# VectorE in the order of the source over a whole two-layer encoder

## The chip, the cores and the metric

One core of one Trainium2 chip runs one program that holds the whole two-layer encoder. The time is that of the device in microseconds (us), from launch to end. Weights are read from HBM as float32 and each is used as the sum of two rounded parts, so the matrix work is three (sometimes two wider) passes for every product.

## What is computed

A residual stream of 16 learned tokens and 256 tokens (T = 272 columns) of width 2048 goes through two layers:

```
h = RMSNorm(x);  [q|k|v|f|ga|gf] = h @ W_in
a = attention(q, k, v) @ W_attn_br          # 8 heads, 2 key/value heads
s = Re(DFT2(f)) @ W_four                    # fourier branch
x = x + (sigmoid(ga)*a + sigmoid(gf)*s) @ W_out
x = x + W_down( silu(dwconv3(RMSNorm(x) @ W_up_gate)) * (RMSNorm(x) @ W_up_val) )
```

The 16 tokens are dropped at the end. The feed-forward width is 5632.

## The kernel before, in words

All weights pass through one stream of **chunks** of 128x1024 float32 (512 KB each), numbered 0 to 947 in the order of use. For a chunk, SyncE issues the load into a tile `raw` (seven buffers, L264); ScalarE writes the rounded high part `wh` (L300); VectorE writes the rest `wl` = `raw` - `wh` (L303); TensorE reads both. `wh` and `wl` have three buffers each, so at most two chunks lie ready ahead of the one in use, and the two parts of chunk n+3 can be written only when TensorE has read chunk n. The `raw` buffer of chunk n is free when its `wl` is done, and then chunk n+7 can be loaded.

The chunks of one matrix group (`group`, L346) follow each other. Names of groups: `ga`, `gf` (gates, 4 chunks), `s` (fourier branch, 2 chunks), `a` (attention branch, 2), `o` (output projection, 2), `ug` and `uv` (the two halves of the feed-forward's first matrix, 4 each), `d` (its second, 5 or 6). In a normal chunk TensorE does 24 matmuls: for each of 8 weight blocks two that read `wh` and then one that reads `wl` (L372, L373, L374). In layer 1 the feed-forward also has chunks of **products** (`ps_p`, L1415): six matmuls of 512 columns, four that read `wh` and then two that read `wl`. They stand singly, in pairs or in threes between the chunks of `ug` and `uv`.

In layer 0, each of the two chunks of an `s` group is first **folded** on VectorE: half of it is added to and subtracted from the other half (`fold_w`, L291, two instructions, into the single buffer `wpm`), and `wh` and `wl` are made from `wpm`. There are eight such groups.

Behind each `ug` group stands the **conv chain** (`conv_gate`, L1246), for each of the group's two halves m: `u` (VectorE, L1255, frees the accumulator), `cv` (ScalarE, L1257), two steps of the convolution (VectorE, L1259 and L1260), silu (ScalarE, L1261), and in layer 0 a product with the norm (VectorE, L1263):

```
nc.vector.tensor_tensor(hv(u[:, lo:T]), de(ps[m][:, :W]), ...)                     # L1255
nc.scalar.activation(cv[:, lo2:T], u[:, lo2:T], AF.Identity, bias=bc, scale=wc(1)) # L1257
nc.vector.scalar_tensor_tensor(cv[:, a:T], u[:, a - 1:T - 1], wc(0), ...)          # L1259
nc.vector.scalar_tensor_tensor(cv[:, lo2:T - 1], u[:, lo2 + 1:T], wc(2), ...)      # L1260
nc.scalar.activation(cv[:, lo2:T], cv[:, lo2:T], AF.Silu)                          # L1261
nc.vector.tensor_tensor(cv, cv, rstdB, op=ALU.mult)                                # L1263
```

After an `o` group of the second half and after the last `d` groups stands a **norm step** for each of two tiles: the sum into the residual stream (VectorE, L1236 or L1286), the scaled copy and the square (ScalarE, L517 and L523), the low part and the running sum of squares (VectorE, L518 and L527).

The source writes the splits of chunk n+2 between the matmuls of chunk n (`pump`, `advance`), and attention, fourier transforms and norms run as generators that are stepped between the matmuls (`step`). A scheduler then sets the order of the instructions of each engine from the dependencies and its own estimates; the source's order is only its priority. Two stretches (the group `f` 2 of layer 0, and the group `q` 1 with the folded fourier projection of layer 1) are already kept in the order of the source on VectorE. Every engine takes its instructions strictly in the order that it has been given, and waits on semaphores where an operand is not ready.

## Time and profile before

| | before |
|---|---|
| median of three runs | 2420.45 us (2418.58 to 2429.65) |
| the profiled execution's own time | 2423.76 us |
| its span, first to last instruction | 2421.7 us |
| TensorE busy | 2375.5 us, 18992 matmuls |
| VectorE busy | 1818.4 us, 2889 instructions |
| ScalarE busy | 1308.3 us, 1893 instructions |
| mean granted clock of TensorE | 0.994 |

The profile tells each instruction's line, engine and tiles (out<-in, with buffer numbers left out), how long an engine sat idle before it and which engine's instruction ended that wait. A window is a stretch of the span in us from its start. In the windows' table "PE busy" is TensorE and PEclk the share of full speed that its clock was granted.

### The profile page before, as it was taken

What the parts mean: (1) busy time and instruction counts of PE and PEld (TensorE: products, weight loads), DVE (VectorE), ACT (ScalarE), POOL (GpSimd) and SP (SyncE); (2) the same over time, 40 slices, a digit from 0 to 9 for tenths busy, and PEclk for the clock granted to TensorE, in tenths of its full rate; (3) what the DMA queues carried; (4) which work ended last, traced back from release to release, by engine and by line L of the source; (5) the groups of instructions that cost most, each with busy time, mean ns of one, the idle gap of its engine ahead of it and who ended that gap; (6) DMA issues with size and microseconds to landing.
All of it is one profiled execution on the core that took longest, in us unless ns stands there. A gap on an engine that the chain in (4) does not pass through costs nothing.

```text
span 2421.7 us, 47634 instructions
## 1 busy us (share of the span) xinstructions
PE 2375.5 (98%) x18992; PEld 2315.1 (96%) x18992; DVE 1818.4 (75%) x2889; ACT 1308.3 (54%) x1893; POOL 134.0 (6%) x265
## 2 busy tenths in 40 slices
PE   9999899999999999999999999999999999999999
PEld 9999899999999999999998999999989999999988
DVE  7788666687776656677668877766878888878798
ACT  6455444464444434444445655545677566666565
POOL 0000010100000000000000000000000000000000
PEclk9999899999999999999999999999999999999999
DMA  7547898899999999999885646888889989988787
GB/s 276 175 155 237 244 288 264 269 298 309 311 315 335 313 306 333 300 343 319 271 261 166 204 156 196 269 265 271 286 290 312 317 281 318 298 299 277 260 279 251
DMA packets 171215, 660.69 MB, mean 273 GB/s; under 512 B 19424, under 2 KB 24672, under 8 KB 170096
## 3 DMA queue, kind: packets, MB, share of 16 engines
q1 hardware_dynamic: 152528, 538.07, 63.9%
q0 software_dynamic: 17024, 117.45, 19.3%
q8 instruction: 149, 2.44, 0.4%
q10 hardware_dynamic: 1440, 2.13, 0.2%
q14 instruction: 74, 0.61, 0.1%
HBM read 635.91 MB, written 136.31 MB: 319 GB/s over the span
## 4 chain that ended last, share of the span: by engine, by line
PE 88%; DVE 6%; DMA 3%; ACT 2%; issue 1%; POOL 0%; SPq 0%; DVEq 0%; ACTq 0%; POOLq 0%
PE ps_p L1415 9%; PE ps_ug L374 7%; PE ps_ug L373 6%; PE ps_ug L372 6%; PE ps_uv L368 4%; PE ps_d L373 3%; PE ps_uv L374 3%; PE ps_d L372 3%; PE ps_uv L372 3%; PE ps_uv L373 3%; PE ps_d L374 3%; DVE wl L303 3%; PE ps_o L372 2%; PE ps_o L373 2%; PE ps_o L374 2%; PE ps_gf L372 2%
## 5 line engine op out<-in xcount | busy, mean ns | idle before, releaser
L303 DVE TENSOR_TENSOR wl<-raw,wh 128x1024 fp32r<-128x1024 f32 (+1 forms) x937 | 1127.0, 1217 | 460.0 <-ACT wh L300 452.1
L300 ACT CAST wh<-raw 128x1024 fp32r<-128x1024 f32 (+1 forms) x937 | 965.7, 1042 | 762.5 <-PE ps_ug L373 197.9
L374 PE MATMUL ps_ug<-xHL,wl 128*128 128x272 f32 (+1 forms) x1408 | 390.8, 278 | 2.2 <-DVE wl L303 2.1
L372 PE MATMUL ps_ug<-xHL,wh 128*128 128x272 f32 (+1 forms) x1408 | 390.8, 278 | 0.2 <-ACT wh L300 0.2
L373 PE MATMUL ps_ug<-xHL,wh 128*128 128x272 f32 (+1 forms) x1408 | 390.0, 277 | 0.0
L374 PEld LDWEIGHTS ps_ug<-xHL,wl 128*128 128x128 f32 x1408 | 267.5, 190 | 3.3 <-DVE wl L303 3.1
L372 PEld LDWEIGHTS ps_ug<-xHL,wh 128*128 128x128 f32 x1408 | 267.3, 190 | 2.7 <-ACT wh L300 0.6
L373 PEld LDWEIGHTS ps_ug<-xHL,wh 128*128 128x128 f32 x1408 | 267.4, 190 | 2.1
L372 PE MATMUL ps_uv<-xHL,wh 128*128 128x272 f32 x704 | 196.4, 279 | 0.0
L373 PE MATMUL ps_uv<-xHL,wh 128*128 128x272 f32 x704 | 196.4, 279 | 0.0
L374 PE MATMUL ps_uv<-xHL,wl 128*128 128x272 f32 x704 | 196.4, 279 | 0.0
L372 PE MATMUL ps_d<-gHL,wh 128*128 128x272 f32 x704 | 196.4, 279 | 0.0
L373 PE MATMUL ps_d<-gHL,wh 128*128 128x272 f32 x704 | 196.4, 279 | 0.0
L374 PE MATMUL ps_d<-gHL,wl 128*128 128x272 f32 x704 | 196.4, 279 | 0.0
L1415 PE MATMUL ps_p<-wh,opnd 128*128 128x512 f32 x688 | 177.5, 380 | 0.3 <-ACT wh L300 0.3
L374 PE MATMUL ps_ga<-xHL,wl 128*128 128x272 f32 (+1 forms) x512 | 144.9, 283 | 10.9 <-DVE wl L303 10.9
L372 PE MATMUL ps_ga<-xHL,wh 128*128 128x272 f32 (+1 forms) x512 | 146.6, 286 | 4.5 <-DVE se L1207 4.5
L368 PE MATMUL ps_uv<-xHL,wh 128*128 128x512 f32 x448 | 150.8, 383 | 0.1
L372 PE MATMUL ps_gf<-xHL,wh 128*128 128x272 f32 (+1 forms) x512 | 144.9, 283 | 5.1 <-DVE se L1207 4.9
L373 PE MATMUL ps_ga<-xHL,wh 128*128 128x272 f32 (+1 forms) x512 | 144.4, 282 | 0.0
L373 PE MATMUL ps_gf<-xHL,wh 128*128 128x272 f32 (+1 forms) x512 | 143.1, 280 | 0.0
L374 PE MATMUL ps_gf<-xHL,wl 128*128 128x272 f32 (+1 forms) x512 | 143.1, 279 | 0.0
(372 smaller groups left out, 5857.2 us busy)
## 6 DMA issues: line engine op xcount, KB each, us to landing
raw<-in_w_up SPq DMA_DIRECT2D x320, 512.0 KB, 5.6
raw<-in_w_in SPq DMA_DIRECT2D x191, 512.0 KB, 4.5
raw<-in_w_down SPq DMA_DIRECT2D x88, 512.0 KB, 7.0
raw<-ft SPq DMA_DIRECT2D x80, 512.0 KB, 4.8
raw<-in_w_out SPq DMA_DIRECT2D x64, 512.0 KB, 5.7
ft<-in_w_dn POOLq DMA_DIRECT2D x30, 1024.0 KB, 12.3
raw<-in_w_dn SPq DMA_DIRECT2D x60, 512.0 KB, 5.0
raw<-in_w_abr SPq DMA_DIRECT2D x32, 512.0 KB, 4.7
```

Source lines behind the costliest of these rows:

```text
L300: nc.scalar.copy(h[:, a:b], r[:, a:b])
L303: nc.vector.tensor_tensor(lo[:, a:b], r[:, a:b], h[:, a:b].bitcast(F32), op=ALU.subtract)
L368: nc.tensor.matmul(o2, h[:, c, sl], ab, start=kt == 0, stop=False)
L372: nc.tensor.matmul(o, h[:, c, sl], a, start=kt == 0, stop=False)
L373: nc.tensor.matmul(o, h[:, c, sl], b, start=False, stop=False)
L374: nc.tensor.matmul(o, lo[:, c, sl], a, start=False, stop=kt == nk - 1)
L1415: nc.tensor.matmul(st2(ps[h]), x, al(w[:, 512 * h:512 * h + 512]), start=fresh and (s_, q) in BEGIN and first, stop=(s_, q) in END and end ...
```

## The change

One line is put around the call that writes the whole program: VectorE (DVE) takes its instructions in the order in which the source writes them. The orders of TensorE, ScalarE, GpSimd and SyncE are still found by the scheduler, which now sees the fixed order on VectorE.

```
     with tile.TileContext(nc) as tc:
-        encoder_kernel(tc, *args)
+        with tc.manual_schedule(engines={mybir.EngineType.DVE}):
+            encoder_kernel(tc, *args)
```

No instruction is added or taken away; 2493 of VectorE's 2891 instructions stand at another place than before, most of them by fewer than ten places. Three places follow; the numbers behind `wl`, `wh`, `raw` and `wpm` are the chunk's, those behind an underscore the buffer's name.

First, VectorE in layer 0 around the second fourier group `s` 1 (chunks 72 and 73); chunk 80 is the first of the next `s` group, seven chunks later. Before:

```order
L303 TENSOR_TENSOR wl73_3395<-wpm73_3385,wh73_3394 128x1024
L1227 TENSOR_TENSOR th_2123<-th_2123,th_2948 128x272
L1226 SCALAR_TENSOR_TENSOR th_2123<-th_2123,ps_0_a_0_1_3340 128x272
L291 TENSOR_TENSOR wpm80_3633<-raw80_3374 128x512
L1229 TENSOR_TENSOR mL_3338<-th_2123,mH_3337 128x272
L1227 TENSOR_TENSOR th_2123<-th_2123,th_2948 128x272
L303 TENSOR_TENSOR wl74_3427<-raw74_3177,wh74_3426 128x1024
```

and with the change, the same stretch:

```order
L303 TENSOR_TENSOR wl73_3397<-wpm73_3387,wh73_3396 128x1024
L1226 SCALAR_TENSOR_TENSOR th_2125<-th_2125,ps_0_a_0_0_3341 128x272
L1227 TENSOR_TENSOR th_2125<-th_2125,th_2950 128x272
L1229 TENSOR_TENSOR mL_3340<-th_2125,mH_3339 128x272
L1226 SCALAR_TENSOR_TENSOR th_2125<-th_2125,ps_0_a_0_1_3342 128x272
L1227 TENSOR_TENSOR th_2125<-th_2125,th_2950 128x272
L1229 TENSOR_TENSOR mL_3340<-th_2125,mH_3339 128x272
L303 TENSOR_TENSOR wl74_3429<-raw74_3179,wh74_3428 128x1024
```

and, further on, the place to which the fold of chunk 80 went:

```order
L303 TENSOR_TENSOR wl79_3599<-raw79_3343,wh79_3598 128x1024
L1184 TENSOR_TENSOR th_3620<-ps_0_gf_3_0_3495,rstdB_82 128x272
L1184 TENSOR_TENSOR th_3620<-ps_0_gf_3_1_3496,rstdB_82 128x272
L291 TENSOR_TENSOR wpm80_3635<-raw80_3376 128x512 x2
L303 TENSOR_TENSOR wl80_3645<-wpm80_3635,wh80_3644 128x1024
L291 TENSOR_TENSOR wpm81_3671<-raw81_3420 128x512 x2
```

The fold of chunk 80 stood ahead of the low part of chunk 74; now it stands behind that of chunk 79, next to the split of chunk 80 itself.

Second, VectorE in the feed-forward of layer 0, behind `ug` group 5 (its last chunk is 211; 212 and 213 are the two that lie ready, 214 is the next). Before:

```order
L303 TENSOR_TENSOR wl213_8310<-raw213_8071,wh213_8309 128x1024
L1255 TENSOR_TENSOR u_8331<-ps_0_ug_5_0_8201,rstdB_80 128x272
L1255 TENSOR_TENSOR u_8339<-ps_0_ug_5_1_8202,rstdB_80 128x272
L1259 SCALAR_TENSOR_TENSOR cv_8333<-u_8331,prm_71,cv_8333 128x271
L1260 SCALAR_TENSOR_TENSOR cv_8333<-u_8331,prm_71,cv_8333 128x271
L303 TENSOR_TENSOR wl214_8361<-raw214_8102,wh214_8360 128x1024
L1263 TENSOR_TENSOR cv_8333<-cv_8333,rstdB_80 128x272
```

and with the change:

```order
L303 TENSOR_TENSOR wl213_8312<-raw213_8073,wh213_8311 128x1024
L1255 TENSOR_TENSOR u_8333<-ps_0_ug_5_0_8203,rstdB_82 128x272
L1259 SCALAR_TENSOR_TENSOR cv_8335<-u_8333,prm_73,cv_8335 128x271
L1260 SCALAR_TENSOR_TENSOR cv_8335<-u_8333,prm_73,cv_8335 128x271
L1263 TENSOR_TENSOR cv_8335<-cv_8335,rstdB_82 128x272
L1255 TENSOR_TENSOR u_8341<-ps_0_ug_5_1_8204,rstdB_82 128x272
L1259 SCALAR_TENSOR_TENSOR cv_8343<-u_8341,prm_73,cv_8343 128x271
L1260 SCALAR_TENSOR_TENSOR cv_8343<-u_8341,prm_73,cv_8343 128x271
L1263 TENSOR_TENSOR cv_8343<-cv_8343,rstdB_82 128x272
L303 TENSOR_TENSOR wl214_8363<-raw214_8104,wh214_8362 128x1024
```

The low part of chunk 214 stood in the middle of the chain of the first half; now the whole chain of both halves stands ahead of it.

Third, ScalarE in the feed-forward of layer 1, behind `ug` group 2 (its last chunk is 636, the next are 637 and 638, both products, and 639, of `uv`). Its order is the scheduler's in both. Before:

```order
L300 CAST wh638_23208<-raw638_23024 128x1024
L1257 ACTIVATE cv_23232<-u_23230,prm_71 128x256
L300 CAST wh639_23252<-raw639_23043 128x1024
L1257 ACTIVATE cv_23239<-u_23237,prm_71 128x256
L1261 ACTIVATE cv_23232<-cv_23232 128x256
L300 CAST wh640_23264<-raw640_23073 128x1024
```

and with the change:

```order
L300 CAST wh638_23210<-raw638_23026 128x1024
L1257 ACTIVATE cv_23234<-u_23232,prm_73 128x256
L300 CAST wh639_23254<-raw639_23045 128x1024
L300 CAST wh640_23266<-raw640_23075 128x1024
L1261 ACTIVATE cv_23234<-cv_23234 128x256
L1257 ACTIVATE cv_23241<-u_23239,prm_73 128x256
```

The cast of chunk 640 moved ahead of the second half's `cv`, for which VectorE's chain waits; on VectorE the low part of chunk 639, which stood behind the first half's L1260, now stands behind the second half's.

## The prediction

> **What bounds the kernel now.** The page first.

> ```profile
> span 2421.7 us, 47634 instructions
> ...
> PE 2375.5 (98%) x18992; PEld 2315.1 (96%) x18992; DVE 1818.4 (75%) x2889; ACT 1308.3 (54%) x1893; POOL 134.0 (6%) x265
> ```

> TensorE (PE) is busy for all but 46 us, so it is the bound, and a change on VectorE (DVE) can only take away TensorE's waits or add to them. Where they lie is shown by the windows by stage (three of the fourier groups in layer 0, then the feed-forward of layer 0 and of layer 1; columns as named in the first row):

> ```profile
> core 0: us, PE busy (x) PEld busy (x) DVE busy (x) ACT busy (x) POOL busy (x), PEclk, DMA share, GB/s
> 242.00:302.50 60.50, 51.09 (x402) 50.77 (x401) 40.63 (x70) 25.13 (x40) 4.91 (x10) 0.89 0.84 245
> 363.00:423.50 60.50, 55.25 (x450) 54.84 (x448) 37.21 (x64) 26.89 (x39) 4.22 (x10) 0.94 0.84 264
> 423.50:484.00 60.50, 54.84 (x457) 54.64 (x458) 41.71 (x64) 27.01 (x41) 8.10 (x12) 0.97 0.88 267
> 541.00:1155.00 614.00, 614.00 (x5302) 613.96 (x5302) 417.83 (x625) 284.59 (x353) 41.00 (x88) 1.00 0.96 318
> 1755.00:2421.70 666.70, 658.90 (x4261) 606.84 (x4259) 553.76 (x707) 429.39 (x556) 17.76 (x26) 1.00 0.86 289
> ```

> Of the 46 us, 20.3 (9.4 + 5.25 + 5.65) lie in the three fourier windows, where the clock was also granted below 1. The feed-forward of layer 0 loses nothing, that of layer 1 7.8 us in 667. The waits say who is late:

> ```profile
> PE ps_ga L374 <- DVE wl L303: 10.9, 3, 4.9
> PE ps_gf L372 <- DVE se L1207: 4.9, 1, 4.9
> ```

> ```profile
> DVE wpm L291 <- DMA raw<-in_w_four: 29.5, 7, 7.6
> ```

> TensorE's longest waits, up to 4.9 us each, end on VectorE, which had waited for loads in front of folds (up to 7.6 us). Its other waits, for casts, are the normal rhythm: TensorE frees a buffer, ScalarE casts, VectorE subtracts.

> **The change part by part.** *The folds.* VectorE's time line around `s` 1:

> ```profile
> 241.42 1.30 DVE L291 TENSOR_TENSOR wpm<-raw 128x512 f32<-128x512 f32 x2
> ...
> 250.03 0.69 DVE L291 TENSOR_TENSOR wpm<-raw 128x512 f32<-128x512 f32 x1 [4.20 <-DMA raw<-in_w_four]
> ```

> The fold at 250.03 is that of chunk 80, seven chunks early; its load could start only when the fold at 241.42 had freed a `raw` buffer. Behind it are queued the low part of chunk 74 (three rows further in the order) and the evacuation of `s` 1 (`se`), for which TensorE stands still. In the new order the fold stands behind the split of chunk 79, four chunks of TensorE work later, so this wait goes in all its places. It is worth 20.3 us of idle time and, in lost clock, up to 12.1 us (60.5 x (0.11 + 0.06 + 0.03)), partly inside the idle time: between 20 and 32, taken as 30, since the clock comes back only after matmuls have resumed.

> What is late next: the early fold was also a head start. Now fold, cast, subtract follow each other twice on VectorE, 2 x (1.30 + 1.03 + 1.22) = 7.1 us (cast and subtraction as in the rows at 654.20 and 655.28 below), against two chunks and a bit, 5.6 + 0.8. Where the buffer comes free in time this leaves 0.5 us late (3 of 8 groups), behind another evacuation of 0.9 us 1.4 (5 groups); where an `a` group's evacuation of some 3.4 us (six steps and two casts of about 0.43) stands ahead of the next low part, another 2.1 (3 groups). Sum 1.5 + 7 + 6.3 = 15. Folds together: -15, between -32 and +5.

> *The conv chain in layer 0*, 22 times. The group shown in the order, before, on VectorE, ScalarE and TensorE (start, duration, line, tiles; in brackets the wait ahead and its end):

> ```profile
> 653.21 0.43 DVE L1255 TENSOR_TENSOR u<-ps_ug,rstdB 128x272 f32<-128x272 f32 x1
> ...
> 654.33 0.50 DVE L1259 SCALAR_TENSOR_TENSOR cv<-u,prm,cv 128x271 f32<-128x271 f32 x1
> 654.87 0.50 DVE L1260 SCALAR_TENSOR_TENSOR cv<-u,prm,cv 128x271 f32<-128x271 f32 x1
> 655.28 1.22 DVE L303 TENSOR_TENSOR wl<-raw,wh 128x1024 fp32r<-128x1024 f32 x1
> 656.42 0.44 DVE L1263 TENSOR_TENSOR cv<-cv,rstdB 128x272 f32<-128x272 f32 x1
> ```

> ```profile
> 653.68 0.62 ACT L1257 ACTIVATE cv<-u,prm 128x272 f32<-128x272 f32 x1 [1.70 <-DVE u L1255]
> 654.20 1.03 ACT L300 CAST wh<-raw 128x1024 fp32r<-128x1024 f32 x1
> 655.14 0.61 ACT L1257 ACTIVATE cv<-u,prm 128x272 f32<-128x272 f32 x1
> 655.65 0.42 ACT L1261 ACTIVATE cv<-cv 128x272 f32<-128x272 f32 x1
> ```

> ```profile
> 653.63 0.28 PE L372 MATMUL ps_uv<-xHL,wh 128*128 128x272 f32 x1
> ```

> A matmul takes 614 / 5302 = 0.116 us, a chunk of 24 takes 2.78. `uv` begins at 653.63, so chunk 214's low part is first read two chunks and two matmuls later, at 653.63 + 5.56 + 0.23 = 659.4. It was ready at 656.5, 2.9 us early. In the new order VectorE first runs the chain of both halves, and waits inside it. From the first half's L1260, which ends at 655.37 as before: silu 655.8, L1263 656.25, `u` 656.6, `cv` (ScalarE) 657.3, L1259 and L1260 658.35, silu 658.8, L1263 659.25, then the low part, 1.22, at 660.4 or so: TensorE waits 1.0 us. That is with ScalarE free when it is wanted. In 10 of the 22 groups its order has chunk n+3's cast ahead of the first `cv` and chunk n+4's ahead of the second. The latter must wait until TensorE has read chunk n+1 (653.63 + 2.78 + 0.05 = 656.45). Then the first `cv` ends at 655.3, L1263 at 657.3, the cast at 657.8, the second `cv` at 658.35, L1263 at 660.3, the low part at 661.45: 2.0 us late. Sum 10 x 2.0 + 12 x 1.0 = 32 us. Bounds: 12, if the chain starts half a microsecond earlier or finds ScalarE free; 45, if the prefold's steps (0.42 each) stand in it everywhere.

> *The conv chain in layer 1.* `ug` group 2, before:

> ```profile
> 1827.25 1.23 DVE L303 TENSOR_TENSOR wl<-raw,wh 128x1024 fp32r<-128x1024 f32 x1
> 1828.39 0.48 DVE L1259 SCALAR_TENSOR_TENSOR cv<-u,prm,cv 128x256 f32<-128x256 f32 x1
> ```

> ```profile
> 1826.19 1.03 ACT L300 CAST wh<-raw 128x1024 fp32r<-128x1024 f32 x1
> 1827.12 0.60 ACT L1257 ACTIVATE cv<-u,prm 128x256 f32<-128x256 f32 x1
> 1827.63 0.41 ACT L1261 ACTIVATE cv<-cv 128x256 f32<-128x256 f32 x1
> ```

> ```profile
> 1825.75 1.03 PE L1415 MATMUL ps_p<-wh,opnd 128*128 128x512 f32 x4
> ...
> 1827.05 1.03 PE L1415 MATMUL ps_p<-wh,opnd 128*128 128x512 f32 x4
> ...
> 1828.56 0.35 PE L369 MATMUL ps_uv<-xHL,wl 128*128 128x256 f32 x1
> ```

> A product's chunk lasts 1.30 us (1825.75 to 1827.05), so two of them leave little lead: chunk 639's low part was done at 1828.48 and was read at 1828.56. In the new order it stands behind the second half's L1260. ScalarE: cast 639 until 1827.2, then cast 640 (its buffer is read until 1826.8) until 1828.2, silu 1828.55, second `cv` 1829.1; VectorE: L1259 and L1260 (0.48 each) until 1830.1, low part at 1831.3. That is 2.7 us late. The 22 groups differ in the two chunks that follow and in ScalarE's order: least where a long chunk follows (1.1), most where cast 639 also stands ahead of the first `cv` (4.2); the eight groups without `uv` have about 2 us more lead and four more steps of 0.42. Taken as 2.7 for 21, 1.5 for the first: 58 us, between 25 and 90. The 14 `uv` evacuations (copy, two steps, twice) come in front of the next low part in the same way, about 0.65 each: 9. VectorE is also the busiest here, 553.76 of 666.7, so there is little slack to catch up in.

> *The norm steps.* Before, two `o` groups stand 5.56 us apart (491.17 to 496.73):

> ```profile
> 491.17 0.43 DVE L1236 SCALAR_TENSOR_TENSOR XT<-ps_o,XT 128x272 f32<-128x272 f32 x1
> ...
> 496.73 0.43 DVE L1236 SCALAR_TENSOR_TENSOR XT<-ps_o,XT 128x272 f32<-128x272 f32 x1
> ```

> In order, each half is 0.43, a wait of about 0.5 for ScalarE (as its small steps in the rows above), and two steps of about 0.45; the two low parts of 1.22 follow. That is near 6, taken as 5.9 since instructions that follow each other overlap by about 0.1: 0.35 longer; 16 groups, and 8 of `d` at 0.6: 10 us, between 0 and 15.

> *The other shadow work* (attention, the branches of layer 1). Its chains move forward by about three places, so VectorE waits for ScalarE where it now does something else:

> ```profile
> DVE rs L1083 <- ACT pe L1078: 9.2, 14, 1.1
> ```

> Of 36 such places 14 wait now, 0.66 each; all 36 would add 15 us, half of it covered: 8, and 4 for three evacuations of layer 1. Taken as 12, between -5 (TensorE also gets these results sooner) and 25.

> *The clock.* In the first window 9.4 us of idle time, nearly all in two waits near the longest, cost 6.7 us of clock (60.5 x 0.11) on top, 3.3 each, while the feed-forward of layer 0, without waits, was granted 1.00. Of the new waits only some six, of 4 us, come near those: 10 us with some uncertainty, half their 20.

> [...]

> Sum: -15 + 32 + 58 + 9 + 10 + 12 + 10 = +116. The profiled execution took 2423.76 us (span 2421.7 and 2.1 around it), so 2540; it lies 3.3 above the median, so 2537.

> **The rivals.**
> - *Faster.* The waits at the folds go and the chains stay hidden, because the two chunks that lie ready cover them. For it: layer 0 had 2.9 us to spare. Against it: layer 1 had 0.08, and the chain grows by more than either. It decides where the low part of chunk n+3 ends before it is read. Time: 2420.45 - 30 + 10 = 2400.
> - *Half the price.* The chains start earlier than I put them, or ScalarE is free more often: half of 32 + 58 + 9 + 10 + 12, no clock: 2420.45 - 15 + 60 = 2466.
> - *Every wait trips the clock.* If 2.7 us is enough, 22 waits in layer 1 pay 3.3 each, 73 instead of 10: 2600. [...]
> - *Nothing happens*, because the fixed order is what the scheduler had: the order excludes it.

> **How the numbers follow.** Chances: forecast (2490 to 2580) 0.55, half price (2445 to 2490) 0.17, clock or a VectorE that can't catch up (2580 to 2640) 0.18, faster 0.06, no change 0.04. The measurement can tell about 0.5%, 12 us. The range leaves out the faster cases and the far end of the dear one: 2455 to 2610. Faster by over 0.5%: 0.06; within: 0.04; slower: 0.90.

> **What would show it.** Right: in the fourier windows PEclk 1.00 and no wait of VectorE's L291 for a load; TensorE waiting for `wl` (L374, L369, L1415) some 20 times in each feed-forward, 1 to 2 us in layer 0 and 2 to 4 in layer 1, and VectorE's L1259 and L1263 waiting for L1257 and L1261. Wrong: a feed-forward of layer 0 that still lasts 614 us, or one of layer 1 under 690.

## The result, and the profile after

The change makes the kernel slower: the median is 2563.95 us against 2420.65 us, a ratio of 1.0581 with a 95% interval of 1.055 to 1.0611. The profiled execution took 2562.59 us. Medians and ratios are of runs at the usual clock: one run of `only_mix1` below (2486.32 us at a granted clock of 0.944) fell into a slower state and is left out. The page of the changed kernel, and its mean granted clock (0.994 before):

```profile
span 2560.8 us, 47657 instructions
...
PE 2426.1 (95%) x18992; PEld 2334.6 (91%) x18992; DVE 1837.0 (72%) x2889; ACT 1318.9 (52%) x1893; POOL 143.4 (6%) x265
```

```profile
core 0: 2560.8 us, clock 0.987
```

The number of instructions on TensorE and VectorE is the same, and VectorE is busy for about the same time (1837 us, 1818 before). TensorE now stands still for 2560.8 - 2426.1 = 135 us instead of 46, and the clock withholds 0.013 x 2560.8 = 33 us instead of 0.006 x 2421.7 = 15. Together that is about 107 of the 139 us. Part of the rest is lost around the stops: the feed-forward of layer 0 gets 33.1 us longer with 24.7 us of idle time in 26 stops, so each costs 0.3 us more than it stands still. The matmuls there start every 0.116 us but last 0.28, and the first one behind a stop lasts 0.38 (row at 690.71 below).

The stages of the changed kernel: three fourier windows at the times that the prediction shows (the work in them is shifted, since the stage begins 12.6 us later), and then the same matmuls of the two feed-forwards:

```profile
core 0: us, PE busy (x) PEld busy (x) DVE busy (x) ACT busy (x) POOL busy (x), PEclk, DMA share, GB/s
242.00:302.50 60.50, 56.13 (x441) 55.01 (x440) 42.74 (x71) 26.93 (x41) 6.22 (x10) 0.93 0.82 251
363.00:423.50 60.50, 56.62 (x460) 55.60 (x459) 40.04 (x62) 24.62 (x33) 4.60 (x10) 0.95 0.85 267
423.50:484.00 60.50, 57.28 (x470) 56.53 (x470) 40.10 (x61) 26.05 (x37) 6.08 (x11) 0.97 0.88 261
563.24:1210.33 647.09, 622.36 (x5302) 616.08 (x5301) 422.16 (x625) 286.07 (x353) 45.23 (x88) 1.00 0.91 300
1825.14:2560.80 735.66, 678.66 (x4261) 611.95 (x4259) 561.94 (x710) 433.12 (x556) 16.39 (x26) 0.99 0.78 262
```

The feed-forward of layer 0 goes from 614.0 to 647.1 us, that of layer 1 from 666.7 to 735.7. The fourier windows, which the prediction saw freed, still have 11.5 us of idle time in all (181.5 - 170.0) and a clock below 1. TensorE's longest waits (in total, times, longest):

```profile
PE ps_uv L369 <- DVE wl L303: 24.6, 14, 6.8
PE ps_ug L374 <- DVE wl L303: 12.9, 12, 4.4
PE ps_uv L374 <- DVE wl L303: 12.5, 15, 1.1
PE ps_ug L372 <- ACT wh L300: 12.1, 12, 1.1
PE ps_p L1415 <- DVE wl L303: 11.8, 15, 2.0
PE ps_s L408 <- DVE wl L303: 8.9, 11, 0.9
PE ps_s L407 <- ACT wh L300: 7.1, 9, 1.5
```

All are waits for one of the two parts of a chunk. VectorE's waits for loads in front of folds (29.5 us before) are gone. In their place stand the waits inside the conv chain, and one of 4.7 us for a transfer (the swap of the key halves, row at 97.37 in the next section):

```profile
DVE cv L1259 <- ACT cv L1257: 89.9, 88, 5.6
...
DVE cv L1263 <- ACT cv L1261: 25.7, 44, 1.8
```

Each of the 88 first convolution steps now waits for ScalarE, 1.02 us on average (before, six of them did, 3.5 us in all). The group that the prediction followed (layer 0, `ug` 5) on VectorE, and then TensorE's stop:

```profile
684.95 0.50 DVE L1260 SCALAR_TENSOR_TENSOR cv<-u,prm,cv 128x271 f32<-128x271 f32 x1
686.01 0.44 DVE L1263 TENSOR_TENSOR cv<-cv,rstdB 128x272 f32<-128x272 f32 x1 [0.56 <-ACT cv L1261]
...
687.48 0.50 DVE L1259 SCALAR_TENSOR_TENSOR cv<-u,prm,cv 128x271 f32<-128x271 f32 x1 [0.68 <-ACT cv L1257]
688.02 0.50 DVE L1260 SCALAR_TENSOR_TENSOR cv<-u,prm,cv 128x271 f32<-128x271 f32 x1
689.08 0.44 DVE L1263 TENSOR_TENSOR cv<-cv,rstdB 128x272 f32<-128x272 f32 x1 [0.56 <-ACT cv L1261]
689.44 3.49 DVE L303 TENSOR_TENSOR wl<-raw,wh 128x1024 fp32r<-128x1024 f32 x3
```

```profile
690.71 0.38 PE L374 MATMUL ps_uv<-xHL,wl 128*128 128x272 f32 x1 [1.08 <-DVE wl L303]
```

From the end of the first half's L1260 (685.45) to the end of the first low part (689.44 + 1.22 = 690.66; the row merges three of them) it takes 5.21 us, where the prediction had 5.03, and TensorE waits 1.08 us, where it had 1.0.

To see where the 139 us lie, the table takes the start of the first matmul into `ps_ga` and into `ps_ug` and of the last into `ps_d` from each trace, and the end of the program, as the ends of the stages. The columns are the change of each stage's length against the kernel before (us); the rows below the first are the experiments of the next section. Each row is one execution, and stages in which nothing was changed differ by up to 4 us (`fold_keep`, layer 1 to the first gate).

| kernel | layer 0 to first gate (134.9) | branches and `o` (395.6) | feed-forward 0 (734.6) | layer 1 to first gate (120.6) | branches and `o` (357.7) | feed-forward 1 (678.2) |
|---|---|---|---|---|---|---|
| the change | +12.6 | +7.9 | +34.8 | +7.0 | +6.1 | +70.8 |
| only_mix0 | +13.8 | +1.0 | +0.8 | -0.5 | 0.0 | +1.8 |
| only_ffn0 | -0.1 | -0.4 | +33.4 | -0.4 | +0.3 | +2.5 |
| only_mix1 | -0.6 | -2.7 | 0.0 | +7.0 | +6.1 | -0.3 |
| only_ffn1 | -0.1 | +0.1 | 0.0 | -1.3 | 0.0 | +71.1 |
| fold_keep | +0.5 | -19.2 | 0.0 | -3.9 | 0.0 | +1.5 |
| fold_ahead | +0.4 | -25.7 | 0.0 | 0.0 | 0.0 | +0.1 |
| chain_late | +12.9 | +4.3 | +1.6 | +8.1 | +6.1 | +48.0 |
| chain_late2 | +13.2 | +1.7 | +1.6 | +8.0 | +6.1 | +25.4 |
| more_lead5 | +10.0 | -7.4 | +12.3 | +4.7 | +3.9 | +33.4 |
| loads_off | +14.0 | +6.3 | +34.7 | +6.9 | +6.1 | +70.5 |
| act_too | +10.7 | +13.7 | +42.6 | +15.9 | +33.1 | +93.7 |
| all_fixed | +15.5 | -5.0 | +1.6 | +8.7 | +6.1 | +25.8 |

### The profile page after: what moved, and what is told of

Read it like the earlier page. It is cut to its first block, busy times and chain, and to the rows that moved or that the text cites. A ratio compares the mean times of both kernels' runs of the same rounds, so it can differ in the third digit from the quotient of the medians.

```text
span 2560.8 us, 47657 instructions
## 1 busy us (share of the span) xinstructions
PE 2426.1 (95%) x18992; PEld 2334.6 (91%) x18992; DVE 1837.0 (72%) x2889; ACT 1318.9 (52%) x1893; POOL 143.4 (6%) x265
## 5 line engine op out<-in xcount | busy, mean ns | idle before, releaser
L300 ACT CAST wh<-raw 128x1024 fp32r<-128x1024 f32 (+1 forms) x937 | 966.1, 1040 | 827.2 <-PE ps_ug L373 180.1
L303 DVE TENSOR_TENSOR wl<-raw,wh 128x1024 fp32r<-128x1024 f32 (+1 forms) x937 | 1119.4, 1216 | 357.1 <-ACT wh L300 349.5
L372 PE MATMUL ps_ug<-xHL,wh 128*128 128x272 f32 (+1 forms) x1408 | 391.2, 279 | 12.1 <-ACT wh L300 12.1
L374 PE MATMUL ps_ug<-xHL,wl 128*128 128x272 f32 (+1 forms) x1408 | 388.7, 279 | 13.2 <-DVE wl L303 12.9
L374 PEld LDWEIGHTS ps_ug<-xHL,wl 128*128 128x128 f32 x1408 | 266.7, 190 | 18.2 <-DVE wl L303 17.6
L372 PEld LDWEIGHTS ps_ug<-xHL,wh 128*128 128x128 f32 x1408 | 268.0, 190 | 16.7 <-ACT wh L300 14.6
L374 PE MATMUL ps_uv<-xHL,wl 128*128 128x272 f32 x704 | 196.9, 282 | 12.5 <-DVE wl L303 12.5
L372 PE MATMUL ps_d<-gHL,wh 128*128 128x272 f32 x704 | 196.5, 279 | 1.1 <-ACT wh L300 1.1
L374 PE MATMUL ps_d<-gHL,wl 128*128 128x272 f32 x704 | 196.3, 279 | 0.0
L372 PE MATMUL ps_uv<-xHL,wh 128*128 128x272 f32 x704 | 195.9, 279 | 0.0
L1415 PE MATMUL ps_p<-wh,opnd 128*128 128x512 f32 x688 | 178.7, 381 | 1.2 <-DVE res L1337 1.0
L369 PE MATMUL ps_uv<-xHL,wl 128*128 128x256 f32 x448 | 124.4, 285 | 24.8 <-DVE wl L303 24.6
L374 PEld LDWEIGHTS ps_uv<-xHL,wl 128*128 128x128 f32 x704 | 132.1, 189 | 16.6 <-DVE wl L303 15.6
L372 PE MATMUL ps_gf<-xHL,wh 128*128 128x272 f32 (+1 forms) x512 | 145.5, 284 | 1.8 <-DVE se L1207 1.8
L372 PE MATMUL ps_ga<-xHL,wh 128*128 128x272 f32 (+1 forms) x512 | 144.0, 281 | 1.9 <-ACT wh L300 1.1
L374 PE MATMUL ps_o<-mH,wl 128*128 128x272 f32 (+1 forms) x512 | 142.8, 279 | 1.0 <-DVE wl L303 0.8
## 6 DMA issues: line engine op xcount, KB each, us to landing
ft<-in_w_dn POOLq DMA_DIRECT2D x30, 1024.0 KB, 12.3
```

The costliest lines, as they stand in the source:

```text
L300: nc.scalar.copy(h[:, a:b], r[:, a:b])
L303: nc.vector.tensor_tensor(lo[:, a:b], r[:, a:b], h[:, a:b].bitcast(F32), op=ALU.subtract)
L369: nc.tensor.matmul(o, lo[:, c, sl], ab[:, 0], start=False, stop=kt == nk - 1)
L372: nc.tensor.matmul(o, h[:, c, sl], a, start=kt == 0, stop=False)
L374: nc.tensor.matmul(o, lo[:, c, sl], a, start=False, stop=kt == nk - 1)
L1415: nc.tensor.matmul(st2(ps[h]), x, al(w[:, 512 * h:512 * h + 512]), start=fresh and (s_, q) in BEGIN and first, stop=(s_, q) in END and end ...
```

## The experiments

**The four parts alone.** The fixed order is put around one of the four blocks of the program, in the kernel before; the same edit four times, on the pool of the mixing block or of the feed-forward, for `l == 0` or `l == 1`:

```diff
-        with tc.tile_pool(name=f"mix{l}", bufs=1) as mp:
+        with tc.tile_pool(name=f"mix{l}", bufs=1) as mp, tc.manual_schedule(engines={mybir.EngineType.DVE}) if l == 0 else ExitStack():
```

> VectorE in source order only in the mixing block of layer 0 (attention, fourier branch, gates, output projection). Theory 'by place': the stage lengths of the two traces add up (first gate +14.4 us later, fourier stage +5.6, second half of the output projection +2.0), so about 2443 us. Rival 'the folds pay as predicted': -15 for the folds and +4 to +8 for the rest, so about 2412 us; then the lengthening in the full change was brought in from elsewhere.

> VectorE in source order only in the feed-forward of layer 0. Theory 'the chain of the conv gate stands ahead of the low parts': 22 groups with one TensorE wait of 1.1 to 1.7 us each, +33 us and +1 for the down projection, so about 2455 us, with a granted clock of 1.00 in this stage. Rival 'the chain only costs because the program enters the stage late or with shuffled buffers': under 2440 us.

> VectorE in source order only in the mixing block of layer 1. Theory 'by place': +8 us in k, v, q and the folded f, +2 in the branches, +3 in the output projection, so about 2434 us. Rival 'these small waits are taken up by slack when the neighbours keep the scheduler's order': within 5 us of the kernel before.

> VectorE in source order only in the feed-forward of layer 1. Theory 'the chain ahead of the low parts, with little lead, and clock': about +69 us as in the full change, so 2490 us, with five spells of half clock. Rival 'part of it is a backlog of earlier stages': under 2470 us. The four parts should add up to the 143 us of the full change within about 15 us; if they don't, the parts act on each other.

Measured, against 2422.78 for the kernel before: 2440.5 (ratio 1.0066, interval 1.0044 to 1.0089), 2457.94 (1.0147, 1.0132 to 1.0163), 2437.26 (1.0059, 1.004 to 1.0079) and 2492.93 (1.0291, 1.0275 to 1.0306). The four differences add up to 17.7 + 35.2 + 14.5 + 70.2 = 137.5 us, beside 143 for the whole change. The table shows the same by stage: each part lengthens its own stages, by about what the change lengthens them, and leaves the others alone within 3 us. The exception is the branches of layer 0, +1.0 alone and +7.9 in the change, which was not explained. The cost is paid place by place; there is no backlog. The feed-forwards alone:

```profile
540.62:1187.96 647.34, 622.32 (x5303) 616.08 (x5301) 421.95 (x625) 286.12 (x353) 45.23 (x88) 1.00 0.90 300
```

```profile
1753.71:2491.50 737.79, 682.73 (x4261) 615.82 (x4259) 561.71 (x710) 433.10 (x556) 16.39 (x26) 0.98 0.78 261
```

**The folds alone.** In the kernel before, only the folds are held where the source has them (`fold_keep`). In `fold_ahead` they are held one chunk earlier, with two buffers for `wpm` and, to make room, six for `raw`:

```diff
-            nc.vector.tensor_tensor(r[:, o:o + 2], raws[i][:, 0:2], raws[i][:, 2:4], op=op)
+            tc.keep_in_program_order(nc.vector.tensor_tensor(r[:, o:o + 2], raws[i][:, 0:2], raws[i][:, 2:4], op=op))
```

```diff
-    RAW, LOOK = 7, 2
+    RAW, LOOK = 6, 2
...
-            if i in folded:
-                todo.append((i, lambda i=i: fold_w(i)))
             for a in (0, 2) if i <= 3 else (0,):
                 todo.append((i, lambda i=i, a=a: split_w(i, a, a + 2 if i <= 3 else CW)))
+            if i + 1 in folded:
+                todo.append((i, lambda i=i: fold_w(i + 1)))
...
-        r = wp.tile([P, CW, MG * P], F32, tag="wpm", name=f"wpm{i}", bufs=1)
+        r = wp.tile([P, CW, MG * P], F32, tag="wpm", name=f"wpm{i}", bufs=2)
```

> The kernel before with the folds alone held where the source has them. Prediction on record: the waits for loads go (30 us), the lost head start costs 15, so about 2407 us. Theory from the changed kernel's trace: with one wpm buffer fold, cast and low part of the two folded chunks follow each other in series, TensorE waits twice at each of the eight s groups (about 24 us) and the clock is tripped about as often, so the gain is given back at once: 2415 to 2428 us.

> The kernel before with the folds held one chunk ahead of the place that the source gives them, with two wpm buffers instead of one (and six raw buffers instead of seven, to make room). Theory 'series through one wpm buffer': neither the waits for loads nor the waits at the s groups are left, so 20 us of idle time and most of the four clock spells of this stage go: about 2395 us. Rival 'the folds cost VectorE time wherever they stand, or six raw buffers make loads late': 2415 us or more.

Measured, against 2424.46: `fold_keep` 2402.08 us (ratio 0.9902, interval 0.9885 to 0.9919), `fold_ahead` 2397.04 (0.9882, 0.9867 to 0.9897). Both are faster than either kernel of the study. The expectation's theory, that the gain is given back at once, falls; the prediction's own term, -15, had the sign and two thirds of the size of the -22 measured. The fourier windows of `fold_keep`, and TensorE's waits at the `s` groups in `fold_keep` and then in `only_mix0`:

```profile
242.00:302.50 60.50, 57.92 (x491) 56.86 (x490) 51.05 (x89) 30.81 (x50) 6.93 (x12) 1.00 0.90 277
363.00:423.50 60.50, 60.14 (x520) 59.94 (x519) 44.24 (x71) 29.00 (x42) 5.90 (x14) 1.00 0.95 301
423.50:484.00 60.50, 59.78 (x515) 59.38 (x514) 48.54 (x81) 32.98 (x51) 6.21 (x12) 1.00 0.96 300
```

```profile
PE ps_s L408 <- DVE wl L303: 4.3, 8, 0.7
PE ps_s L407 <- ACT wh L300: 2.0, 5, 1.1
```

```profile
PE ps_s L408 <- DVE wl L303: 8.0, 10, 0.9
PE ps_s L407 <- ACT wh L300: 5.9, 8, 1.5
...
PE ps_s L407 <- DVE th L1226: 1.9, 3, 0.6
```

With the folds alone in place the clock is 1.00 in all three windows and the idle time 3.7 us (181.5 - 177.8), and the lost head start costs 6.3 us of waits at the `s` groups. When everything else is put in order too, these waits are 15.8 us and the clock dips again. So in the change the gain of the folds is there, and is eaten in the same stage by what was moved with them. One part of this is visible: ScalarE's order stays the scheduler's, but is another one; it now has the cast of the fourier groups' small 64-row weights where their load has not landed, in the change

```profile
ACT w L384 <- DMA r<-in_w_f: 25.9, 8, 6.3
```

and for three groups that stands ahead of the cast of the first folded chunk. The kernel before has 1.2 us of such waits, `fold_keep` 0.5, `only_mix0` 22.6 in five. What they cost TensorE was not separated.

**The conv chain written otherwise.** Everything in source order, as in the change, but the source leaves the taps (L1259 to L1261) and the product with the norm (L1263) to later steps, two steps after the evacuations `u`. In `chain_late` this is done for all groups of layer 0 and the 14 with `uv` of layer 1; `chain_late2` does it for the other eight too, and also leaves the evacuations of `uv` and the products of the eight groups without `uv` to such steps:

```diff
+                    cs.append(cv)
+                    us.append((u, wc))
-                    nc.vector.scalar_tensor_tensor(cv[:, a:T], u[:, a - 1:T - 1], wc(0), cv[:, a:T], op0=ALU.mult, op1=ALU.add)
...
+                def rest():
+                    for x, cv in zip(us, cs):
+                        taps(x, cv)
+                        yield 1
...
+                push(rest(), 2)
                 return cs
```

> VectorE in source order everywhere, as in the change, but the source of the conv gate emits the two evacuations first and leaves the taps of each half to later steps, so that a low part stands between; in layer 1 this is done for the 14 groups with uv and not for the 8 others. Theory 'the chain stands ahead of the low part': the feed-forward of layer 0 loses most of its 33 us of waits and that of layer 1 about half of its 69: near 2500 us. Rival 'a fixed order of VectorE costs what it costs, whichever source order it fixes': within 15 us of 2564.

> As chain_late, and in layer 1 also the groups without uv and the evacuations that follow (uv, products of the eight pairs) are left to later steps. Theory 'in the feed-forward of layer 1 it is whatever is written as one block ahead of the next low part': the 48 us left there fall to 20 or less, so about 2475 us. Rival 'VectorE, the busiest here after TensorE, has no room for a fixed order': they stay above 40, about 2500 us.

Measured: 2504.78 us against 2424.46 (ratio 1.0327, interval 1.031 to 1.0344), and 2481.52 against 2420.8 (1.0253, 1.0224 to 1.0283). The same windows of the feed-forwards, `chain_late` first:

```profile
559.95:1173.87 613.92, 613.92 (x5303) 613.92 (x5302) 419.09 (x625) 286.71 (x353) 42.65 (x88) 1.00 0.96 317
1789.78:2502.70 712.92, 675.12 (x4261) 609.60 (x4259) 560.91 (x710) 432.46 (x556) 16.52 (x26) 0.99 0.80 271
```

```profile
1787.36:2477.70 690.34, 666.96 (x4261) 605.55 (x4259) 558.95 (x710) 431.54 (x556) 16.33 (x26) 1.00 0.84 279
```

The feed-forward of layer 0 is back at 613.9 us: all of its 33 us came from the chain standing as one block ahead of a low part. In layer 1 the two edits take away 23 and then 23 more of the 69 us. The rival, that a fixed order costs what it costs, is out for all of layer 0's loss and two thirds of layer 1's; 24 us of layer 1 stay, a little more than the 20 expected.

**One more chunk of lead.** As the change, with four `wh` and `wl` buffers and, to make room, five `raw` buffers:

```diff
-    RAW, LOOK = 7, 2
+    RAW, LOOK = 5, 3
...
-            splits[i] = tuple(wp.tile([P, CW, MG * P], F32R, tag=t, name=f"{t}{i}") for t in ("wh", "wl"))
+            splits[i] = tuple(wp.tile([P, CW, MG * P], F32R, tag=t, name=f"{t}{i}", bufs=4) for t in ("wh", "wl"))
```

> VectorE in source order everywhere, as in the change, with one more chunk split ahead (four wh and wl buffers, LOOK 3; raw buffers 5 instead of 7 to make room). Theory 'the low part comes 1 to 3 us late against two chunks of lead': one more chunk of 2.78 us covers the waits of the feed-forward of layer 0 (-33) and 1.30 us more of a product about half of layer 1 (-30): near 2500 us. Rival 'VectorE falls behind for good': within 15 us of 2564.

Measured 2489.85 us (ratio 1.0267, interval 1.025 to 1.0285). The windows of its feed-forwards:

```profile
548.10:1169.89 621.79, 616.76 (x5302) 615.75 (x5301) 419.65 (x625) 286.94 (x354) 50.40 (x88) 1.00 0.93 312
1783.99:2478.50 694.51, 665.16 (x4261) 606.35 (x4259) 557.33 (x709) 429.46 (x555) 16.39 (x26) 1.00 0.81 278
```

A lead of one more chunk takes 25 of 33 us in layer 0 and 41 of 69 in layer 1, with the chain still written as one block. It is lateness against a fixed lead, as the prediction had it, not a VectorE that can't keep up.

**Two loads at the heads of queues.** As the change, with the evacuations of `v` ahead of the drain, and each small 64-row weight loaded when the one before it has been used:

```diff
-            if not last:
-                drain()
             vt = mp.tile([P, NKV, 3 * P], F32, tag="q2b" if last else "q2", name="vt")
...
+            if not last:
+                drain()
...
         nc.vector.tensor_tensor(w[64:96], r[32:64], w[32:64].bitcast(F32), op=ALU.subtract)
+        if i < NG - 1:
+            load_w64(l, i + 1)
```

> The changed kernel with two engine queues freed of a load: in layer 0 the evacuations of v stand ahead of the drain that emits the rest of the key path (VectorE waited there 4.7 us for the swap of the keys), and the small 64-row weights of each fourier group are loaded right after the previous ones are used (ScalarE waited 25.9 us in eight places for them, three times ahead of the cast of the first folded chunk). Theory 'a fixed VectorE runs into loads at two queue heads': about -6 us before the first gate (4.4 of waiting and a clock spell) and about -10 us in the branch stage of layer 0, so near 2548 us. Rival 'what is queued behind them was late anyway': within 5 us of 2564.

Measured 2562.26 us against 2420.8 (ratio 1.0584, interval 1.0569 to 1.06): nothing gained. VectorE in the changed kernel, and TensorE's longest wait of this stage there and then here:

```profile
97.37 0.73 DVE L928 TENSOR_TENSOR qs<-qs,cst 128x544 f32<-128x544 f32 x1 [4.69 <-DMA qs<-kp]
...
100.84 0.43 DVE L983 TENSOR_TENSOR vt<-ps_v,rstdB 128x272 f32<-128x272 f32 x1
```

```profile
PE ps_vt L991 <- DVE vt L983: 4.2, 1, 4.2
```

```profile
PE ps_q L374 <- DVE wl L303: 7.8, 6, 4.5
```

The first half of the expectation failed because the low part is behind the same wait: with `vt` out of the way TensorE stops 4.5 us for `wl` instead. The second half was not tested at all: SyncE's order is the scheduler's, the load went out at the same time (403.6 us in one trace, 403.9 in the other), and ScalarE still waited 25.5 us for it. What the 64-row weights cost is left open.

**ScalarE in source order too.**

```diff
-        with tc.manual_schedule(engines={mybir.EngineType.DVE}):
+        with tc.manual_schedule(engines={mybir.EngineType.DVE, mybir.EngineType.Activation}):
             encoder_kernel(tc, *args)
```

> ScalarE in the order of the source too. Theory 'the waits come from the source order itself, which puts a whole chain ahead of the next split': the feed-forwards get no better, since the casts too now stand behind both halves of the chain, and ScalarE waits at the 64-row weights right where they are loaded: 2580 to 2640 us. Rival 'the waits come from ScalarE's planned order not fitting VectorE's fixed one': the feed-forwards lose a good part of their 104 us, under 2530.

Measured 2632.13 us (ratio 1.0869, interval 1.0853 to 1.0885). The feed-forwards lose 8 and 23 us more, the branches of layer 1 27 more. TensorE's longest waits are now for casts, first of all in `uv` of layer 1:

```profile
PE ps_uv L368 <- ACT wh L300: 28.6, 13, 4.7
```

So the mismatch of a planned ScalarE and a fixed VectorE is not what costs; with the planned ScalarE the loss is the smaller one. The expected waits for the 64-row weights did not appear.

**All edits of the source together.**

> VectorE in source order with every edit of the source tried so far: taps and evacuations of the feed-forwards in later steps, folds one chunk ahead with two wpm buffers (six raw buffers), evacuation of v ahead of the drain, early load of the 64-row weights. Theory 'the loss is the source's order, place by place': the gains add up, 2475 - 16 - 20 = about 2440 us, near the kernel before and above fold_ahead's 2397. Rival 'a fixed order loses to the scheduler's everywhere by a little': 2470 us or more.

It joins the diffs of `chain_late2`, `loads_off` and the folds of `fold_ahead` (without holding them one by one, since all of VectorE is held). Measured 2479.2 us (ratio 1.0239, interval 1.0223 to 1.0256): the rival's number. In the branches of layer 0 the folds one chunk ahead, together with the early loads, are worth 6.7 us here (+1.7 in `chain_late2` to -5.0) where the folds were worth 25.7 with the scheduler's order around them.

## Why the prediction was right, and where not

The forecast of +116 us stands beside +143 measured (+139 between the two traces). The mechanism that carries it, the conv chain, is shown by experiment for layer 0 and for two thirds of layer 1. The two feed-forwards came out at 34.8 + 70.8 = 105.6 us, where the terms that lie there are 32 + 58 + 9, 4.8 of the norm steps and most of the clock's 10. Nearly all that is missing lies outside them: 33.6 us measured, where the folds (-15), the other shadow work (12) and the norm steps behind `o` (5.6) come to 3. That the sum is no further off is partly luck, since it was too high in one place and too low in the other. By the prediction's own steps:

- *The folds* (-15, between -32 and +5): right when they are moved alone, -22. The waits for loads went, the head start cost 6.3 us of waits where I had 8.5 for the groups themselves (1.5 + 7). In the change, the stage got 8 us longer all the same. The 6.3 us that I put down for evacuations ahead of the next low part, together with the 8 of the attention, was the step that failed, by 14 against more than 20: in `only_mix0` the rest of the order costs this stage 20 us more than the folds alone (+1.0 against -19.2), 12 of it idle (the gaps ahead of matmuls in this stage sum to 21.0 us against 9.0) and the rest clock and short waits.
- *The conv chain in layer 0* (32 us): 33.1, at 22 groups. The lateness was as forecast: behind the chain the low part ends 6.9 to 7.0 us after the start of `uv` in 11 groups and 7.9 to 8.3 in the other 11, which is 1.1 to 1.2 and 2.1 to 2.5 us later than the 5.79 (5.56 + 0.23) at which it would be read; the prediction had twelve groups of 1.0 and ten of 2.0. But TensorE doesn't pay it in that way. The groups of the first kind cost 1.3 us each, a stop of about 1.05 and the restart. In those of the second kind the scheduler, which knew the fixed order, gave TensorE another one: 52 matmuls of `uv`, four of the next group, then the other 44 of `uv`. The four stand still 1.1 us for a cast, which ScalarE has behind the second half's silu, and the group costs 1.5 to 1.9 us in all. At `uv` of 635.67, on ScalarE and TensorE:

```profile
641.89 1.03 ACT L300 CAST wh<-raw 128x1024 fp32r<-128x1024 f32 x1
```

```profile
642.97 0.38 PE L372 MATMUL ps_ug<-xHL,wh 128*128 128x272 f32 x1 [1.11 <-ACT wh L300]
```

So the sum came out for the right reason, with the two kinds less far apart on TensorE than on VectorE. In `chain_late` every `uv` is one run of 96 matmuls again and the stops are gone, which shows the cause.
- *The conv chain and `uv` in layer 1* (58 + 9) and its share of the clock: 69 measured for the whole stage. Idle time there is 57 us (735.7 - 678.7), 49 more than before, so the waits were set some 18 us too high: there are 49 stops, 8 of them of 2 us or more, where I had 22 of about 2.7. Half clock (six steps of 3.413 us, 10 us withheld) and the restarts made up for it. The written order accounts for 45 us by `chain_late2`; the last 24 were not separated. One stop is of another kind, on ScalarE, VectorE and TensorE:

```profile
1863.58 1.04 ACT L300 CAST wh<-raw 128x1024 fp32r<-128x1024 f32 x1 [4.18 <-DMA raw<-fv]
```

```profile
1865.46 0.48 DVE L1259 SCALAR_TENSOR_TENSOR cv<-u,prm,cv 128x256 f32<-128x256 f32 x1 [5.63 <-ACT cv L1257]
```

```profile
1867.65 0.80 PE L369 MATMUL ps_uv<-xHL,wl 128*128 128x256 f32 x2 [6.79 <-DVE wl L303]
```

ScalarE has a cast whose load is late ahead of the chain's `cv`, VectorE must wait for that `cv`, and a low part behind it, whose operands were ready, makes TensorE wait 6.8 us. In the kernel before, ScalarE waits for the same load, but it has already done the second half's `cv`, and VectorE gets two more low parts done before that cast:

```profile
1787.40 0.60 ACT L1257 ACTIVATE cv<-u,prm 128x256 f32<-128x256 f32 x1
...
1792.01 1.05 ACT L300 CAST wh<-raw 128x1024 fp32r<-128x1024 f32 x1 [2.76 <-DMA raw<-fv]
```

- *The norm steps* (10): no experiment separates them. Those behind the eight groups of `d` lie, nearly all, in the feed-forward of layer 0, where all that is left without the chain is 1.6 us, against the 4.8 that I had for them.
- *The other shadow work* (12): too low. Layer 0 up to the first gate costs 12.6 to 13.8 us, layer 1 up to its first gate 7.0, its branches 6.1, all reproduced by the parts alone; with the branches of layer 0 it is the largest miss. I had counted ScalarE's round trips and not the drain of the key path, in which VectorE waits for the swap: a stop of 4.2 us and a spell of half clock at it (3.4 us withheld) are in the trace of the change and not in that of before. `loads_off` didn't take them away, so that they come from this wait alone is not shown.
- *The clock* (10): 19 us more withheld. There are 13 spells of half clock instead of 5, six of them in the fourier stage, which I had seen free of them, and five in the feed-forward of layer 1.
- *The rivals.* "Faster" had the folds right and the chains wrong. "Half the price" (2466) is near what remains when the chains are written otherwise, but not what the change does. "Every wait trips the clock" did not happen: the 22 waits of layer 0 leave its clock at 1.00, and the 49 of layer 1 brought five spells.
- *What would show it*: the waits for `wl` and inside the chain appeared, in layer 0 with the 1 to 2 us told, but half of them for the cast; in layer 1 with 0.2 to 6.8 us instead of 2 to 4, and twice as often as told. PEclk 1.00 in the fourier windows was wrong for the change, right for the folds.

Open: the 13 us before the first gate of layer 0, the 13 of layer 1 ahead of its feed-forward and the 20 us around the folds, which no new order in the source took away (one more chunk of lead takes 15 us out of the branches of layer 0, +7.9 to -7.4), and the last 24 us of layer 1's feed-forward.

## What to carry to other kernels

In this kernel some 78 of the 139 us (33 in layer 0, 45 in layer 1) were the price of what the source writes as a block, with waits for another engine inside, ahead of work that the busiest engine needs next. Such a block can be priced from the rows of the trace, in layer 0 within 1 us of 33, where the lead and the waits inside are regular; in layer 1 the waits were set 18 us too high. Look for the one instruction that the scheduler puts too early and hold that one: the folds alone, held one chunk ahead of their place in the source, gave 1.2%, while holding all of VectorE lost 5.8%. The moved steps of a stage must be priced together, since a gain at one can be eaten in the same stage by another.

## What the hardware showed that was not expected

```profile
451.62:455.03 3.41, 2.06 (x14) 1.51 (x12) 2.52 (x3) 0.71 (x2) 1.08 (x2) 1.00 0.32 127
455.03:458.40 3.37, 1.50 (x10) 1.30 (x11) 2.40 (x4) 2.67 (x4) 0.00 (x0) 1.00 0.90 311
458.40:461.80 3.40, 3.40 (x18) 3.40 (x17) 2.64 (x7) 1.53 (x4) 0.00 (x0) 0.50 0.82 258
```

A wait of 1.46 us, of which 1.0 lies in the second step, and one of 0.88 leave 3.37 - 1.50 = 1.87 us of it idle, and the third step runs at half clock. In `only_mix1` a single wait of 3.10 us fell across a step's end, 1.84 and 1.26 us idle, and the clock stayed:

```profile
454.90:458.30 3.40, 1.56 (x14) 1.36 (x12) 1.23 (x3) 1.04 (x1) 0.00 (x0) 1.00 0.54 192
458.30:461.70 3.40, 2.14 (x18) 2.14 (x19) 3.40 (x5) 0.00 (x0) 0.93 (x1) 1.00 0.63 182
461.70:465.10 3.40, 3.40 (x31) 3.40 (x31) 2.09 (x4) 1.88 (x3) 0.94 (x2) 1.00 0.86 287
```

Over the 14 traces (the kernel before, the change and the twelve experiments), of the steps at full clock with 1.9 us idle or more 85 of 86 were followed by half clock, of those with 1.0 to 1.9 us 23 of 244, and of some 9600 with less none, the ends of the programs left out (in the kernel before and the change alone: 16 of 16, 2 of 41, none of 1368). In the change, the 26 stops in the feed-forward of layer 0, of 1.12 us at most, left its clock at 1.00, while in the fourier stage all six spells follow pairs or rows of waits of 0.2 to 1.5 us.
